# A decoder trunk with eight routed experts: four experts in 64 columns and two weight passes, heavy and light experts interleaved

## The chip, the cores and the metric

The kernel runs on one core of a Trainium2 chip. The metric is the device time of one execution in microseconds (us), as a median of several runs. The engines are named as the profile names them: PE is the tensor engine's matmul and PEld its weight load, DVE the vector engine, ACT the scalar engine, POOL the GpSimd engine, SP the engine whose queue issues nearly all transfers.

## The reference, cut to what matters

Two layers, each a mixer and then a feed-forward part, on 256 tokens of width 1024 in float32. The feed-forward part of layer 0 is dense, that of layer 1 is a mixture of eight experts of which each token takes two:

```
logits = t @ w_router                              # 256 x 8
top_v, top_i = top_k(logits, 2)
gates = sum(one_hot(top_i, 8) * softmax(top_v)[..., None], axis=1)
for e in range(8):
    out += gates[:, e:e+1] * ((silu(t @ w_g[e]) * (t @ w_u[e])) @ w_d[e])
```

Each expert has w_g and w_u of 1024 x 2816 and w_d of 2816 x 1024, 33 MiB in all. The 512 choices of the reference's own inputs fall on experts 0 to 7 as 60, 83, 83, 61, 59, 56, 66 and 44 tokens.

## The kernel before

The mixers and the dense part come first; the expert loop begins when the router has run, and takes most of the time.

**Precision.** A float32 product is made of three matmuls in the type fp32r. Every operand is split into a high part (a rounded copy, made by ACT) and a low part (what is left over, made by DVE); `mm3` (L158) then adds high x high, high x low and low x high into one PSUM bank.

**Blocks.** Weights come in blocks of 1 MiB (128 partitions x 2048 floats), 33 to an expert: 11 for gate, 11 for up, 11 for down. `weights` (L129) does everything for one block in the order of the program: a transfer on SP's queue into one of up to twelve buffers, ACT's copy `wr` (L117) and DVE's remainder `wl` (L119). Both `wr` and `wl` are in a pool `ring` of three buffers, so the split of a block can begin only when PE has finished the block three before it:

```
ring = ctx.enter_context(tc.tile_pool(name="ring", bufs=3))
```

One block feeds twelve matmuls of 512 columns (the last chunk's gate and up blocks feed 24 of 256).

**An expert.** `gather` (L714) picks the tokens of a pair of experts by matmuls with one-hot matrices, 128 columns to each expert, and splits the picked columns. `up` (L752) runs over six chunks c of the hidden width (five of 512, one of 256): tokens are the stationary operand (128 x 128), weights the moving one. ACT takes the SiLU of gate (`s`, L769), DVE multiplies it with up (`hh`, L771). One chunk later `turn` (L774) transposes `hh` on PE and splits it into `hr` and `hl`, and `down` (L785) multiplies with w_d into two banks that live for the whole expert. At the end `scale` (L799) applies the gate factor and `finish` (L809) scatters the rows back into `h` (`cb` L816 on PE, an addition L818 on DVE).

**Order.** The loop (L834) takes experts 0 to 7 and chunks 0 to 5 in order; between the gate half and the up half of a chunk it calls `turn` for the chunk before, after the up half `down`. Engines run their queues in order. A block that runs only if an expert has more than 128 tokens (`rest`, L852) is not entered with these inputs.

Of the kernel before, what the change touches and what calls it, by code (L numbers as in the profile page):

```python
# [16 lines left out]
P = 128  # L17
# [6 lines left out]
NE = 8  # L24
EPS = 1e-6
LEVELS = (64, 32, 16, 8, 4, 2, 1)
NL = len(LEVELS) + 1

# [6 lines left out]
K_ID, K_IOTA, K_LT, K_PAR = 0, 128, 384, 448  # L35
# [8 lines left out]
def small_arrays(i):  # L44
# [13 lines left out]
    c[:, K_LT:K_LT + NE * NE] = (e[None, :] < e[:, None]).reshape(1, -1)  # L58
    masks = np.zeros((P, NL, P), np.float32)
# [45 lines left out]
def trunk_kernel(ctx: ExitStack, tc: tile.TileContext, x, w_in, w_out, dense_w_gate, dense_w_up, dense_w_down,  # L105
# [62 lines left out]
    def tmp(shape, name, tag="tmp", bufs=5, dt=F32):  # L168
        pool = area["scratch"] if tag in ("tmp", "u", "cf_acc", "S", "r", "v", "gy", "qk", "sx") else sb
        return pool.tile(shape, dt, name=name, tag=tag, bufs=3 if tag == "tmp" and area["spare"] else bufs)  # L170
# [16 lines left out]
    iota, lt = kc[:, K_IOTA:K_IOTA + T], kc[:, K_LT:K_LT + NE * NE]  # L187
    wrt = kc[:, K_RT:K_M].rearrange("p (k e) -> p k e", e=NE)
# [431 lines left out]
    def moe(l, j, accs):  # L620
# [58 lines left out]
        gr = tmp([P, TT, NE, 2], "gr", tag="rt_g", bufs=1)  # L679
        nmax = tmp([P, 1], "nmax", tag="rt_n", bufs=1, dt=I32)  # L680

        def gates():
# [18 lines left out]
        X = {}  # L701

        def factors(p):
            oh = X[p][2]
            b = bank([P, 2, 2], "rgb")
            for i in range(2):
                for tt in range(TT):
                    nc.tensor.matmul(b[:, i], oh.bitcast(F32)[:, tt, i], gr[:, tt, 2 * p + i],
                                     start=(tt == 0), stop=(tt == TT - 1))
            rg = tmp([P, 2, 2], "rg", tag="rg", bufs=2)  # L710
            nc.vector.tensor_copy(rg, b)
            X[p].append(rg)

        def gather(p):  # L714
            oh = tmp([P, TT, 2, P], "oh", tag="oh", bufs=1, dt=F32R)
            for tt in range(TT):
                for i in range(2):
                    e = 2 * p + i
                    put = nc.vector.tensor_scalar(oh[:, tt, i], iota[:, 0:P], pos[:, tt, e:e + 1], None, op0=ALU.is_equal)
            xgr, xgl = pair("xg", "A" if p % 2 == 0 else "E")  # L720
            for k2 in range(KT // 2):
                b = bank([P, 2, 2 * P], "gb")
                for i in range(2):
                    kt = 2 * k2 + i
                    n = 0
                    for tt in range(TT):
                        for xs in (xr, xl):
                            nc.tensor.matmul(b[:, i], xs[:, tt, kt * P:(kt + 1) * P], oh[:, tt],  # L728
                                             start=(n == 0), stop=(n == 3))
                            n += 1  # L730
                for i in range(2):
                    kt = 2 * k2 + i
                    last = split(b[:, i], xgr[:, kt], xgl[:, kt], scale=col(R_FFN + KT * l + kt))
            X[p] = [xgr, xgl, oh]
            if p == 0:
                hold(2, (msk_set, last_x), (put,))
                with behind((put,)):
                    gates()
            else:
                factors(p)  # L740

        def back(p):
            oh = X[p][2]
            pt = tmp([P, 2, T], "pt", tag="pt", bufs=1, dt=F32R)
# [5 lines left out]
            X[p].append(pt)  # L750

        def up(e, c, mid):  # L752
            xgr, xgl = X[e // 2][0:2]
            ss = slice((e % 2) * P, (e % 2 + 1) * P)
            n = 512 if c < 5 else 256
            kn = 2048 // n
            bs = []
            for src in (gw, uw):
# [3 lines left out]
                for k0 in range(0, KT, kn):  # L762
                    wr, wl = weights(src[e, 2 * c + k0 // kn], kn, n)
# [3 lines left out]
            rg = X[e // 2][3][:, e % 2, 1:2]  # L767
# [220 lines left out]
```

## Time and profile before

| what | value |
|---|---|
| median of 3 runs | 1246.97 us (1246.82 to 1247.52) |
| the profiled execution | 1244.85 us, of which its span is 1242.7 us |
| mean granted PE clock | 0.994 of full speed |
| busy in the span: PE, DVE, ACT | 1212.8, 1009.7, 795.2 us |
| first and last matmul of gate or up in the expert loop | 444.2 and 1219.6 us |

The span is the time from the first to the last instruction that the profiler recorded. Busy times of different engines overlap. PE's busy time comes from matmuls whose ends are modelled: a matmul of 0.39 us overlaps the next one, which starts sooner than that.

### The profile page before, as it was taken

What the parts mean: (1) busy time and instruction counts of PE and PEld (TensorE: products, weight loads), DVE (VectorE), ACT (ScalarE), POOL (GpSimd) and SP (SyncE); (2) the same over time, 40 slices, a digit from 0 to 9 for tenths busy, and PEclk for the clock granted to TensorE, in tenths of its full rate; (3) what the DMA queues carried; (4) which work ended last, traced back from release to release, by engine and by line L of the source; (5) the groups of instructions that cost most, each with busy time, mean ns of one, the idle gap of its engine ahead of it and who ended that gap; (6) DMA issues with size and microseconds to landing.
All of it is one profiled execution on the core that took longest, in us unless ns stands there. A gap on an engine that the chain in (4) does not pass through costs nothing.

```text
span 1242.7 us, 17120 instructions
## 1 busy us (share of the span) xinstructions
PE 1212.8 (98%) x6897; PEld 1047.1 (84%) x6897; DVE 1009.7 (81%) x1032; ACT 795.2 (64%) x754; POOL 20.4 (2%) x31
## 2 busy tenths in 40 slices
PE   7999999999899999999999999999999999999996
PEld 6998999999899878888888888887787888888885
DVE  5987655555798778889889888888888898888986
ACT  6634543434554677777777777777777777677673
POOL 2000000000000000000000000000000000000000
PEclk9999999999999989999999999999999999999998
DMA  8434454545344769979799999899999899999971
GB/s 359 153 141 153 169 200 175 199 174 172 132 150 174 289 233 368 368 275 367 294 363 364 360 360 343 329 348 361 346 353 366 316 338 388 346 355 367 366 264 36
DMA packets 48788, 348.44 MB, mean 280 GB/s; under 512 B 5431, under 2 KB 5431, under 8 KB 6976
## 3 DMA queue, kind: packets, MB, share of 16 engines
q1 hardware_dynamic: 48384, 345.49, 74.2%
q0 software_dynamic: 320, 1.80, 0.4%
q8 instruction: 56, 0.92, 0.3%
q14 instruction: 28, 0.23, 0.0%
HBM read 346.23 MB, written 1.05 MB: 279 GB/s over the span
## 4 chain that ended last, share of the span: by engine, by line
PE 94%; DVE 4%; issue 1%; ACT 0%; DMA 0%; POOL 0%; POOLq 0%; SPq 0%; DVEq 0%
PE gu L160 16%; PE gu L161 16%; PE gu L159 16%; PE acc_y L160 9%; PE acc_y L159 9%; PE acc_y L161 9%; DVE wl L119 3%; PE gb L728 1%; PE tb L777 1%; PE sbk L417 1%; PE cb L816 1%; PE a_ps L166 1%; PE db L374 1%; PE vb L159 1%; PE vb L160 1%; PE vb L161 1%
## 5 line engine op out<-in xcount | busy, mean ns | idle before, releaser
L117 ACT ACTIVATE wr<-w 128x2048 fp32r<-128x2048 f32 (+2 forms) x273 | 403.9, 1496 | 224.5 <-issue 109.0
L119 DVE TENSOR_TENSOR wl<-w,wr 128x2048 fp32r<-128x2048 f32 (+2 forms) x273 | 475.8, 1765 | 77.4 <-ACT wr L117 77.2
L160 PE MATMUL gu<-wl,xg 128*128 128x512 f32 (+1 forms) x768 | 289.0, 376 | 2.5 <-DVE wl L119 2.4
L159 PE MATMUL gu<-wr,xg 128*128 128x512 f32 (+1 forms) x768 | 288.8, 376 | 0.0
L161 PE MATMUL gu<-wr,xg 128*128 128x512 f32 (+1 forms) x768 | 286.0, 372 | 0.0
L119 DVE TENSOR_TENSOR wl<-wx,wr 128x2048 fp32r<-128x2048 f32 x112 | 253.9, 2288 | 27.4 <-ACT wr L117 27.4
L117 ACT ACTIVATE wr<-wx 128x2048 fp32r<-128x2048 f32 x112 | 214.6, 1917 | 53.7 <-PE gu L161 26.4
L160 PE MATMUL acc_y<-wl,hr 128*128 128x512 f32 x440 | 174.8, 397 | 0.0
L161 PE MATMUL acc_y<-wr,hl 128*128 128x512 f32 x440 | 173.6, 394 | 0.0
L160 PEld LDWEIGHTS gu<-wl,xg 128*128 128x128 f32 x768 | 144.8, 188 | 29.2 <-DVE wl L119 5.7
L159 PE MATMUL acc_y<-wr,hr 128*128 128x512 f32 x440 | 166.1, 395 | 0.0
L159 PEld LDWEIGHTS gu<-wr,xg 128*128 128x128 f32 x768 | 144.7, 188 | 25.4
L161 PEld LDWEIGHTS gu<-wr,xg 128*128 128x128 f32 x768 | 144.7, 188 | 24.5
L160 PEld LDWEIGHTS acc_y<-wl,hr 128*128 128x128 f32 x440 | 82.8, 188 | 21.6 <-DVE wl L119 3.6
L161 PEld LDWEIGHTS acc_y<-wr,hl 128*128 128x128 f32 x440 | 82.9, 189 | 18.5
L159 PEld LDWEIGHTS acc_y<-wr,hr 128*128 128x128 f32 x440 | 82.6, 189 | 18.2
L159 PE MATMUL gu<-f,wr 128*128 128x256 f32 x336 | 95.1, 283 | 0.0
L160 PE MATMUL gu<-f,wr 128*128 128x256 f32 x336 | 95.0, 283 | 0.0
L161 PE MATMUL gu<-f,wl 128*128 128x256 f32 x336 | 95.0, 283 | 0.0
L160 PEld LDWEIGHTS gu<-f,wr 128*128 128x128 f32 x336 | 64.4, 192 | 0.4
L159 PEld LDWEIGHTS gu<-f,wr 128*128 128x128 f32 x336 | 64.4, 192 | 0.4
L161 PEld LDWEIGHTS gu<-f,wl 128*128 128x128 f32 x336 | 64.4, 192 | 0.0
(269 smaller groups left out, 1418.5 us busy)
## 6 DMA issues: line engine op xcount, KB each, us to landing
w<-in_moe_w_up_dram SPq DMA_DIRECT2D x52, 1024.0 KB, 7.2
w<-in_moe_w_down_dram SPq DMA_DIRECT2D x47, 1024.0 KB, 7.1
w<-in_moe_w_gate_dram SPq DMA_DIRECT2D x44, 1024.0 KB, 7.1
wx<-in_moe_w_gate_dram SPq DMA_DIRECT2D x39, 1024.0 KB, 7.2
wx<-in_moe_w_down_dram SPq DMA_DIRECT2D x39, 1024.0 KB, 7.3
wx<-in_moe_w_up_dram SPq DMA_DIRECT2D x34, 1024.0 KB, 7.1
w<-in_w_in_dram SPq DMA_DIRECT2D x20, 1024.0 KB, 4.9
w<-in_dense_w_gate_dram SPq DMA_DIRECT2D x11, 1024.0 KB, 4.9
```

The costliest lines, as they stand in the source:

```text
L117: i0 = nc.scalar.activation(r, src, AF.Copy, scale=scale)
L119: i1 = nc.vector.tensor_tensor(l, src, r.bitcast(F32), op=ALU.subtract)
L159: nc.tensor.matmul(o, sr, mr, start=start, stop=False)
L160: nc.tensor.matmul(o, sr, ml, start=False, stop=False)
L161: nc.tensor.matmul(o, sl, mr, start=False, stop=stop)
L166: nc.tensor.matmul(o, s[:, kt], m[:, kt], start=(n == 0 and kt == 0), stop=(n == 2 and kt == KT - 1))
L374: nc.tensor.matmul(db[:, o0:o1], la_t[n], mst[:, s0:s0 + o1 - o0], start=(n == 0), stop=(n == 1))
L417: nc.tensor.matmul(o, a0, a1, start=True, stop=True)
L728: nc.tensor.matmul(b[:, i], xs[:, tt, kt * P:(kt + 1) * P], oh[:, tt], start=(n == 0), stop=(n == 3))
L777: nc.tensor.transpose(b[:, i], hh[:, i * P:(i + 1) * P], ident)
L816: nc.tensor.matmul(cb, pt[:, e % 2, ts(tt)], ys[:, nh], start=(n == 0), stop=(n == 1))
```

## The change

On the chip, experts 1 to 7 are ranked by their token counts (`places`, 20 small DVE operations after two matmuls). The four with the fewest tokens become light; expert 0 and the other three are heavy. Places 0, 2, 4, 6 of the list hold heavy experts and 1, 3, 5, 7 light ones; place 0 is always expert 0. SP loads the expert number of each place from 1 to 7 into a register, and transfers take their address from it.

A light expert has 64 columns. Its stationary operand holds the high halves of 64 tokens beside the low halves, 128 columns in all. Two matmuls with `wr` and `wl` take the place of three, and the rows of the high and low halves come out apart. ACT copies gate and up from PSUM (`kept`); PE then multiplies each 128 columns of `kept` with `fold`, a 128 x 64 float32 matrix that adds the two halves, transposes them and applies the norm factor; SiLU, product and split follow on 64 columns.

Items are now pairs (place, chunk): three heavy ones first, then heavy and light ones in turn, three light ones last. The down product of a light item is put between the gate and the up half of the next light item. The temporary buffers `tmp` go from three to two. The fallback `rest` runs if a light expert has over 64 tokens or a heavy one over 128. The diff, cut:

```
+FEW = 64
+RANKS = (-1, 0, 4, 1, 5, 2, 6, 3)
+LAG = 3
...
-        return pool.tile(shape, dt, name=name, tag=tag, bufs=3 if tag == "tmp" and area["spare"] else bufs)
+        return pool.tile(shape, dt, name=name, tag=tag, bufs=2 if tag == "tmp" and area["spare"] else bufs)
...
+        def places():
             nb = bank([P, NE], "nb")
             for tt in range(TT):
                 nc.tensor.matmul(nb, oner, msk[:, tt], start=(tt == 0), stop=(tt == 1))
-            nc.vector.tensor_reduce(nmax, nb, axis=AX.X, op=ALU.max)
+            cnt = tmp([P, NE], "cnt", tag="rt_b", bufs=1)
+            nc.vector.tensor_copy(cnt, nb)
...
+            rank = tmp([P, NE], "rank", tag="rt_r", bufs=1)
+            nc.vector.tensor_reduce(rank, w0[:, :, 1:NE], axis=AX.X, op=ALU.add)
+            nc.vector.memset(rank[:, 0:1], -1.0)
...
+            for tt in range(TT):
+                for src, dst in ((pos[:, tt], placed[:, tt]), (gr[:, tt, :, 0], gp[:, tt, :, 0])):
+                    nc.vector.tensor_tensor(w0, to, src[:, None, :].broadcast_to([P, NE, NE]), op=ALU.mult)
+                    nc.vector.tensor_reduce(dst, w0, axis=AX.X, op=ALU.add)
...
+        def which(p):
+            expert[p] = nc.values_load(ids[0:1, p:p + 1], engines=(mybir.EngineType.SP,), min_val=0, max_val=NE - 1,
+                                       skip_runtime_bounds_check_because="a sum of one-hot rows times 0 to 7")
+
+        def block(src, p, n):
+            if p == 0:
+                return src[0, n]
+            return src[bass.ds(expert[p], 1), n].rearrange("e p n -> (e p) n")
...
+        def pick(p, c0, c1):
+            xg, oh = X[p][0:2]
             for k2 in range(KT // 2):
...
-                            nc.tensor.matmul(b[:, i], xs[:, tt, kt * P:(kt + 1) * P], oh[:, tt],
+                            nc.tensor.matmul(b[:, i, c0:c1], xs[:, tt, kt * P:(kt + 1) * P],
+                                             oh[:, tt].rearrange("p a b -> p (a b)")[:, c0:c1],
                                              start=(n == 0), stop=(n == 3))
...
+                    if c0 == 0:
+                        last = split(b[:, i, 0:P], xg[:, 0, kt], xg[:, 1, kt], scale=gain)
+                    if c1 > P:
+                        last = split(b[:, i, P:P + FEW], xg[:, 2, kt, 0:FEW], xg[:, 2, kt, FEW:P], scale=gain)
...
+                fold = tmp([P, FEW], "fold", tag="fold", bufs=2)
+                nc.vector.tensor_scalar(fold, folded, rg[:, 1:2], None, op0=ALU.mult)
...
         def up(e, c, mid):
...
-                        mm3(bs[-1], xgr[:, kt, ss], xgl[:, kt, ss], wr[:, i], wl[:, i], kt == 0, kt == KT - 1)
+                        if e % 2 == 0:
+                            mm3(bs[-1], xg[:, 0, kt], xg[:, 1, kt], wr[:, i], wl[:, i], kt == 0, kt == KT - 1)
+                        else:
+                            nc.tensor.matmul(bs[-1], xg[:, 2, kt], wr[:, i], start=(kt == 0), stop=False)
+                            nc.tensor.matmul(bs[-1], xg[:, 2, kt], wl[:, i], start=False, stop=(kt == KT - 1))
+                if e % 2 == 1:
+                    kept.append(tmp([P, n], "kept", tag="kept", bufs=2))
+                    nc.scalar.activation(kept[-1], bs[-1], AF.Copy)
...
+        def turn(e, c, hh, n):
...
+            b = bank([P, 2, nk, FEW], "fb")
+            for n in range(2):
+                for i in range(nk):
+                    nc.tensor.matmul(b[:, n, i], hh[n][:, i * P:(i + 1) * P], fold, start=True, stop=True)
+            s = tmp([P, nk, FEW], "s")
+            nc.scalar.activation(s, b[:, 0], AF.Silu)
+            nc.vector.tensor_tensor(s, b[:, 1], s, op=ALU.mult)
+            hb = tmp([P, nk, 2, FEW], "hb", tag="hr", bufs=2, dt=F32R)
+            area["turn"] = split(s, hb[:, :, 0], hb[:, :, 1])
...
+                    else:
+                        hb = hr[:, 2 * k2 + i].rearrange("p a b -> p (a b)")
+                        nc.tensor.matmul(Y[e][nh], hb, wr[:, i, cs], start=first, stop=False)
+                        nc.tensor.matmul(Y[e][nh], hb, wl[:, i, cs], start=False, stop=fin)
...
+        many = [(e, c) for e in range(0, NE, 2) for c in range(6)]
+        little = [(e, c) for e in range(1, NE, 2) for c in range(6)]
+        items = many[:LAG]
+        for a, b in zip(many[LAG:], little):
+            items += [a, b]
+        items += little[len(little) - LAG:]
...
+        def between(k, e, c):
             if (e, c) == (0, 0):
-                factors(0)
+                factors(0, 0)
+            if (e, c) == (0, 1):
+                limits(*places())
+                marks(0, 1)
+                pick(0, P, P + FEW)
+                factors(0, 1)
+                back(0)
+            if k:
+                pe, pc, ph, pn = done[-1]
+                held_back.append((pe, pc, turn(pe, pc, ph, pn)))
                 hold(2, area["turn"])
...
+        def lower(k, e, c, turned):
+            down(e, c, *turned)
+            if c == 5 and e < NE - 1:
+                todo.setdefault(("scale", k + 1), []).append(e)
+                todo.setdefault(("finish", k + 2), []).append((e, 0))
+                todo.setdefault(("finish", k + 3), []).append((e, 1))
...
+        for k, (e, c) in enumerate(items):
+            if c == 0 and e > 0:
+                which(e)
+
+            def mid(k=k, e=e, c=c):
+                ready = list(held_back)
+                held_back.clear()
+                between(k, e, c)
+                for pe, pc, turned in ready:
+                    lower(k, pe, pc, turned)
+
+            hh, n = up(e, c, mid)
+            done.append((e, c, hh, n))
+            for pe, pc, turned in [x for x in held_back if x[0] % 2 == 0]:
+                lower(k, pe, pc, turned)
+            held_back[:] = [x for x in held_back if x[0] % 2 == 1]
+            for pe, tt in todo.pop(("finish", k), ()):
+                finish(pe, (tt,))
+            if c == 5 and e % 2 == 0 and e < NE - 2:
+                p = e // 2 + 1
+                space(p)
+                marks(p, 0)
+                marks(p, 1)
+                pick(p, 0, P + FEW)
+                for i in range(2):
+                    factors(p, i)
+                back(p)
...
-    with tc.If(fullest > P):
+    with tc.If(fullest > 0):
```

## Rows read from the trace of the kernel before

**Rows 1.** The page's head, busy time of PE, and the chain that ended last, by engine.

```profile
span 1242.7 us, 17120 instructions
...
PE 1212.8 (98%) x6897; PEld 1047.1 (84%) x6897; DVE 1009.7 (81%) x1032; ACT 795.2 (64%) x754; POOL 20.4 (2%) x31
...
PE 94%; DVE 4%; issue 1%; ACT 0%; DMA 0%; POOL 0%; POOLq 0%; SPq 0%; DVEq 0%
```

**Rows 2.** Busy time of each engine in the expert loop, as one stretch.

```profile
core 0: us, PE busy (x) PEld busy (x) DVE busy (x) ACT busy (x) POOL busy (x), PEclk, DMA share, GB/s
444.00:1220.00 776.00, 773.46 (x3703) 641.04 (x3703) 679.88 (x447) 569.49 (x405) 0.59 (x1) 1.00 0.90 339
```

**Rows 3.** Timeline of PE, the first and last of 23 consecutive matmuls: start, length.

```profile
642.26 0.40 PE L160 MATMUL gu<-wl,xg 128*128 128x512 f32 x1
...
647.29 0.40 PE L161 MATMUL gu<-wr,xg 128*128 128x512 f32 x1
```

**Rows 4.** Groups by line and form: count, busy us, mean ns, idle before.

```profile
L119 DVE TENSOR_TENSOR wl<-w,wr 128x2048 fp32r<-128x2048 f32 x138 | 312.4, 2287 | 28.4 <-ACT wr L117 28.4
L117 ACT ACTIVATE wr<-w 128x2048 fp32r<-128x2048 f32 x139 | 266.2, 1917 | 63.7 <-PE gu L161 38.1 <-PE acc_y L161 20.5 <-DVE wl L119 1.7
...
L771 DVE SCALAR_TENSOR_TENSOR hh<-gu,rg,s 128x512 f32<-128x512 f32 x40 | 30.0, 749 | 15.6 <-PE gu L161 15.4
...
L119 DVE TENSOR_TENSOR hl<-tb,hr 128x512 fp32r<-128x512 f32 x40 | 27.4, 684 | 1.4 <-ACT hr L117 1.4
...
L117 ACT ACTIVATE hr<-tb 128x512 fp32r<-128x512 f32 x40 | 23.9, 597 | 38.3 <-PE tb L777 38.3
```

**Rows 5.** Timeline of DVE: two remainders back to back, two additions back to back.

```profile
659.01 4.50 DVE L119 TENSOR_TENSOR wl<-w,wr 128x2048 fp32r<-128x2048 f32 x2 [0.52 <-ACT wr L117]
...
668.85 1.28 DVE L818 TENSOR_TENSOR h<-h,cb 128x512 f32<-128x512 f32 x2
```

**Rows 6.** Timeline of ACT through one chunk, with what ended each wait.

```profile
655.99 0.69 ACT L769 ACTIVATE s<-gu,rg 128x512 f32<-128x512 f32 x1 [0.80 <-PE gu L161]
...
657.06 1.92 ACT L117 ACTIVATE wr<-w 128x2048 fp32r<-128x2048 f32 x1
659.18 1.92 ACT L117 ACTIVATE wr<-w 128x2048 fp32r<-128x2048 f32 x1 [0.20 <-PE gu L161]
661.90 1.92 ACT L117 ACTIVATE wr<-w 128x2048 fp32r<-128x2048 f32 x1 [0.81 <-PE gu L161]
664.69 1.92 ACT L117 ACTIVATE wr<-wx 128x2048 fp32r<-128x2048 f32 x1 [0.87 <-PE acc_y L161]
```

**Rows 7.** Chain in order of time: a pair's gather, a chunk's four transposes.

```profile
585.35 3.64 PE gb L728 x32
...
655.96 0.44 PE tb L777 x4
```

**Rows 8.** Timeline of PE, float32 matmuls outside the expert loop.

```profile
373.64 1.11 PE L417 MATMUL sbk<-E 64*128 64x64 f32 x16
...
431.20 3.64 PE L642 MATMUL lb<-wrg,ft 128*128 128x8 f32 x32
```

**Rows 9.** Timeline of DVE, small operations of the router.

```profile
436.06 0.29 DVE L667 TENSOR_REDUCE rk<-cmp 128x16 f32<-128x128 f32 x1
...
438.45 0.17 DVE L684 TENSOR_REDUCE mx<-L 128x2 f32<-128x16 f32 x1
```

**Rows 10.** SP's queue: what its transfers wait for, and one register load.

```profile
SPq L140 <- DVE wl L119: 1012.3, 307, 17.8
...
L954 SPq TENSOR_LOAD <-nmax x1: 482/482/482, 1199.0 to 1199.0; - x1
```

**Rows 11.** Three stretches of the expert loop, columns as in rows 2.

```profile
454.00:1204.00 750.00, 747.46 (x3559) 618.46 (x3559) 661.07 (x426) 548.80 (x387) 0.59 (x1) 1.00 0.93 350
...
1032.00:1040.00 8.00, 8.00 (x38) 6.63 (x36) 6.31 (x4) 6.58 (x5) 0.00 (x0) 1.00 1.01 418
1026.00:1123.00 97.00, 96.50 (x455) 79.11 (x455) 84.98 (x51) 70.81 (x48) 0.59 (x1) 1.00 0.95 364
```

More of the change, by code (lines that the diff above doesn't have):

```diff
@@ L714, in gather @@
-        def gather(p):
-            oh = tmp([P, TT, 2, P], "oh", tag="oh", bufs=1, dt=F32R)
-            for tt in range(TT):
[L717 to L720, printed above, removed]
+            cnt = tmp([P, NE], "cnt", tag="rt_b", bufs=1)
+            nc.vector.tensor_copy(cnt, nb)
+            w0 = cmp[:, 0, 0:NE]
@@ new lines, in moe @@
+        gw, uw, dw = moe_w_gate[j], moe_w_up[j], moe_w_down[j]
+        X, expert = {}, {0: 0}
+        def which(p):
[5 more added lines that the diff above has]
+            return src[bass.ds(expert[p], 1), n].rearrange("e p n -> (e p) n")
@@ L732, in gather, with space, factors @@
                     kt = 2 * k2 + i
[L733 to L740, printed above, removed]
+                    gain = col(R_FFN + KT * l + kt)
+                    if c0 == 0:
+                        last = split(b[:, i, 0:P], xg[:, 0, kt], xg[:, 1, kt], scale=gain)
+                    if c1 > P:
+                        last = split(b[:, i, P:P + FEW], xg[:, 2, kt, 0:FEW], xg[:, 2, kt, FEW:P], scale=gain)
+            return last
+        def space(p):
+            t = tmp([P, 4, KT, P], "xg", tag="A" if p % 2 == 0 else "E", bufs=1, dt=F32R)
+            X[p] = [t, t[:, 3, 0:4].rearrange("p (a b) n -> p a b n", a=TT), {}, t[:, 3, 4:8].rearrange("p (a b) n -> p a (b n)", a=2), {}]
+        def factors(p, i):
+            oh = X[p][1]
+            g = gr if p == 0 and i == 0 else gp
+            b = bank([P, 2], "rgb")
+            for tt in range(TT):
+                nc.tensor.matmul(b, oh.bitcast(F32)[:, tt, i], g[:, tt, 2 * p + i], start=(tt == 0), stop=(tt == TT - 1))
+            rg = tmp([P, 2], "rg", tag="rg", bufs=4)
+            nc.vector.tensor_copy(rg, b)
+            X[p][2][i] = rg
+            if i == 1:
+                fold = tmp([P, FEW], "fold", tag="fold", bufs=2)
+                nc.vector.tensor_scalar(fold, folded, rg[:, 1:2], None, op0=ALU.mult)
+                X[p][4][0] = fold
         def back(p):
-            oh = X[p][2]
-            pt = tmp([P, 2, T], "pt", tag="pt", bufs=1, dt=F32R)
+            oh = X[p][1]
+            pt = X[p][3]
             b = bank([P, 2, T], "ptb")
@@ L772, in up @@
-            return hh, n
-        def turn(hh, n):
-            b = bank([P, n // P, P], "tb")
-            for i in range(n // P):
-                nc.tensor.transpose(b[:, i], hh[:, i * P:(i + 1) * P], ident)
-            hr = tmp([P, n // P, P], "hr", tag="hr", bufs=2, dt=F32R)
-            hl = tmp([P, n // P, P], "hl", tag="hl", bufs=2, dt=F32R)
-            area["turn"] = split(b, hr, hl)
-            return hr, hl, n // P
+            nc.vector.scalar_tensor_tensor(s, bs[1], rg, s, op0=ALU.mult, op1=ALU.mult)
@@ L845, in moe @@
-        down(last[0], last[1], *turn(*last[2:]))
+        space(0)
+        put = marks(0, 0)
+        pick(0, 0, P)
+        hold(2, (msk_set, last_x), (put,))
+        with behind((put,)):
+            gates()
+        many = [(e, c) for e in range(0, NE, 2) for c in range(6)]
[4 more added lines that the diff above has]
+        items += little[len(little) - LAG:]
+        held_back, todo = [], {}
@@ L846, in moe @@
+        ready = list(held_back)
+        k = len(items)
+        pe, pc, ph, pn = done[-1]
+        ready.append((pe, pc, turn(pe, pc, ph, pn)))
+        for pe, pc, turned in ready:
+            lower(k, pe, pc, turned)
+        for key in sorted((q for q in todo), key=lambda q: (q[1], q[0] != "scale")):
+            for v in todo[key]:
+                if key[0] == "scale":
+                    scale(v)
+                else:
+                    finish(v[0], (v[1],))
         low = scale(NE - 1)
```

131 lines of the change are left out of this document (80 added, 51 removed).

## The prediction

> **What bounds the kernel now.** I read the page first. PE is busy for 98% of the span and holds 94% of the chain that ended last [rows 1]. The share is an average over stages, so I took the expert loop alone: in its 776 us PE is busy for 773.5, DVE for 679.9, ACT for 569.5, and the transfers run at 339 GB/s with a share of 0.90; the granted clock is 1.00 of full speed, the 2.4 GHz level [rows 2]. Since matmul ends are modelled, a busy PE need not be a full one, so I checked the pace: 23 matmuls start within 5.03 us, 0.229 us apart without a hole [rows 3]. A heavy block (12 matmuls) thus takes 2.74 us. A chunk of 512 has six blocks and four transposes. PE sets the pace now.
>
> The next question is what PE will wait for when it gets faster. A block costs ACT 1.92 and DVE 2.29 us [rows 4]; back to back two remainders take 4.50, so DVE's pace is 2.21 [rows 5]. The reader should see in ACT's timeline why these engines idle: nearly every `wr` waits 0.2 to 0.9 us for a matmul of PE [rows 6]. That is the ring of three: a slot comes free when PE is done with a block, and then 0.2 (the wait's release) + 1.92 + 2.29 + some 0.1 = 4.5 us pass until PE can use the new block in it, while PE works on the two blocks between. Two heavy blocks last 5.48, so 1.0 us is to spare, and PE does not stall. Two light blocks (8 matmuls, 1.83 us each) last 3.66: the ring is then late. DVE's 2.21 is above 1.83 as well. This is the heart of the forecast.
>
> **The change part by part.** *PE's work.* Four light experts of 33 blocks drop 4 of 12 matmuls: 4 x 33 x 4 x 0.229 = 121 us less. (The 256-column blocks drop 8 of 24 at about half the time each; I count them alike.)
>
> The turn of a light chunk gets dearer. Four transposes take 0.44 us [rows 7]. Now 8 float32 products take their place, with a 128-row, 128-column stationary and 64 moving columns. The trace has none of that form. Float32 products show up as two PE instructions each: the router's 16 products are 32 rows in 3.64 us, 0.11 each with 8 columns; the mixer's 64-column products on half the rows are 16 in 1.11, at most 0.07 apart [rows 8]. I take 0.11, since those use the full 128 rows as `fold` does: 16 x 0.11 = 1.76 per chunk, and per expert 88 x 0.11 - 22 x 0.11 = 7.3, in four experts 29 us. The low end, 0.07, would cost 15 in all, so 14 us less; the high end is PE's pace for 512 columns, 0.229, 42 us more.
>
> The first pair's tokens are now picked in two goes. The gather of a pair is 32 matmuls in 3.64 us [rows 7], and 0.11 is also what the 8-column ones cost, so the second go costs about 3.6. PE's work falls by 121 - 29 - 4 = 88 us.
>
> *The ring.* PE's order follows from the text. Around one heavy item H and one light item L it is: gate HH, fold, up HH, then gate LL, transposes, down LL, up LL, then down HH. So six heavy blocks alternate with six light ones, too long a run for a ring of three to even out. Let t = 0 be the first light matmul; durations are those of [rows 4 to 6]. L1 and L2 are ready (L2 at 1.7). `hh` of the heavy chunk follows on DVE (0.75, to 2.35). L3: its slot is free at 0.2, ACT to 2.1, DVE 2.3 to 4.57; PE is past L2 and the transposes at 4.1 and starts at 4.6. L4: DVE to 6.8, starts then. `hl` of the heavy chunk on DVE to 7.4. L5: DVE to 9.6; L6: to 11.8; the next heavy block: to 14.0. Without waiting PE would be there at 6 x 1.83 + 0.44 = 11.4. So a light run loses 2.6 us, a wait of PE for `wl`. In the heavy run DVE needs 6 x 2.21 + about 0.8 (product and split of 64 columns, half the size of `hh` and `hl`) = 14.1 of 18.2 us and catches up, but cannot lay in more than two blocks. Per chunk pair: 33.8 us before, 29.6 by PE's work, 32.2 with the loss.
>
> 21 light items are interleaved, three of them short (chunk 5). 18 full runs cost 18 x 2.6 = 47. The three short ones (three blocks): L3 is ready at 4.6, `hh` and `hl` add 0.5 and 0.4, the next block is ready at about 7.3 against 5.9, so 1.4 each, 4 in all. The last three items are light alone: a chunk costs DVE 6 x 2.21 + 0.8 = 14.1 against PE's 11.0 + 1.76 = 12.7, together 3. Bounds for a full run: with `hh` and `hl` both outside the chain it loses 2.6 - 1.3 = 1.3. With ACT's extra copies in it (`kept` twice and `hr`, 0.6 to 0.7 each by the SiLU of the same size [rows 6] and `hr` [rows 4]) it loses 2.6 + 2.0 = 4.6.
>
> *The ranking.* `places` is emitted in the middle of item 1, and PE's next work, the pick of the light tokens, needs it. 20 DVE operations on 64 elements lie between 0.17 (16 elements) and 0.29 (128) [rows 9]; at 0.23 and 0.03 between two, 5.2, and with `nb` and the one-hot marks about 6 us of PE standing still. It is 0 if these run earlier, in DVE's idle time; 10 if each waits for the one before it a tenth longer and the pick's splits are waited for too. I take 6. What is queued behind on DVE are the next `wl`; two blocks lie ready, so nothing else is late.
>
> *Additions and scatter.* `yg` falls into heavy runs, where DVE has room. Of each of seven experts one half of `finish` falls at the head of a light run: two additions, 1.28 [rows 5], against PE's four scatter matmuls at 0.23: 0.4 each, 3 in all. The splits of three gathers now stand directly before a light run; against a gather's 3.64 on PE [rows 7] eight of some 0.5 on DVE and the marks are about 1 us more each. I take 6 together; 0 to 12.
>
> *At nothing.* Register loads on SP: seven at 0.48 us; SP spends 1012 us waiting for `wl`, so they hide there [rows 10]; without that cover 3.4 us. ACT gains some 25 us of copies over 569 of 776; what hides them is its wait for PE; what they cost without that is the slower rival below. PSUM: the accumulators of two experts hold four of eight banks all the time, and gate, up and the turn of two items share four; each is held 4 to 9 us of 32. `tmp` with two buffers holds one tile of each kind of item. The fallback: the ranked counts are 44, 56, 59, 61, all within 64.
>
> **Sum.** 88 - 47 - 4 - 3 - 6 - 6 = 22 us off the profiled execution, 1244.85 to about 1223. The median of the runs is 2.1 above that execution, so 1247 - 22 = 1225.
>
> **The rivals.**
>
> *PE's work decides.* If the ring's loss vanishes (blocks of both kinds mixed more finely on PE than I read it), 88 - 12 = 76 goes: 1171; 1160 to 1204 with the bounds. For it: DVE's and ACT's sums still fit. Against it: ACT's wait for a slot in nearly every block [rows 6] and a ring that is not changed.
>
> *Slower: the light run costs more than the third pass gives.* The place is the light run, the mechanism ACT in order: `kept` of gate, `hr` and `kept` of up stand between the `wr` of L4 and of the next heavy block. If each delays DVE fully, the loss is 4.6 a run: 18 x 2.0 = 36 more, 1261. It decides from 2.6 + 22/18 = 3.8 us a run on. For it: a wait of ACT on PE stands before `s` and `hr` already (38.3 us over 40 `hr` [rows 4]). Against it: ACT's block is 0.37 shorter than DVE's, so part of it hides.
>
> *The transfers become the bound.* The part of the loop with steady transfers moves 750 us x 350 GB/s = 262.5 MB; the best stretch of one expert ran at 364 GB/s [rows 11]. If that is all they can do, 721 us remain of 750: 29 less, 1218. Against it: 418 GB/s over 8 us in the same loop with all engines busy [rows 11]; at 376 (350 over the share of 0.93) 698 remain, and they don't bind before 52 us are won. The Trainium skill (HBM Reference, Specifications (TRN2)) gives a core some 358 GB/s when its pair streams too, and more to one alone; by 358 as a cap, 733 us would remain and the time would be 1230. The trace's 418 shows that this cap does not hold here.
>
> *It does not do what it says.* Should a light expert have over 64 tokens, the fallback streams all weights again, over 700 us more (264 blocks of 1.05 MB at 376 GB/s). The counts speak against it.
>
> **How the numbers follow.** The ring-limited gain 50% (1205 to 1240), PE's work 20%, transfers 8%, no change 6%, slower by ACT 14%, fallback 2%. I predict 1225. The range leaves out the lower half of the PE case, half of the slower case and the fallback: 1172 to 1254. About 0.2% (2.5 us) is what a measurement of this kernel can tell from no change. Faster 0.50 + 0.20 + 0.08 = 0.78, same 0.06, slower 0.16.
>
> **What would show it.** In the profile after: L runs of PE with waits for DVE `wl` in every light chunk, some 2.6 us; DVE without idle there, but waiting for ACT, and ACT for PE, in heavy runs; `fb` 16 instructions, 0.11 apart; one stop of PE of about 6 us near 460 before `gb`; transfers at 360 to 370 GB/s. I am wrong if light runs flow without waits (then 1171), if `fb` is much dearer or cheaper, or if PE stops at new places, such as bank waits at gate.

## The result, and the profile after

The changed kernel takes 1296.4 us (four runs, 1296.3 to 1296.5) against 1246.9 us: a ratio of 1.040, 95% interval 1.038 to 1.041. It is slower by 49.5 us, where 22 us faster was forecast; 1225 missed by 71 us, and the range's upper end, 1254, by 42.

The page after, its head, busy time of PE, DVE and ACT, and the chain that ended last:

```profile
span 1294.7 us, 17231 instructions
...
PE 1180.2 (91%) x6633; PEld 996.7 (77%) x6633; DVE 1004.9 (78%) x1098; ACT 806.3 (62%) x834; POOL 20.3 (2%) x31
...
PE 70%; DVE 18%; ACT 5%; issue 5%; DMA 1%; POOL 0%; SPq 0%; ACTq 0%; DVEq 0%; POOLq 0%
```

PE lost its hold on the chain: 70% in place of 94% [rows 1], and DVE's share went from 4% to 18%. The work did fall (6633 matmul rows for 6897). Next the expert loop after, by windows: the whole, an undisturbed stretch, the first gather, the ranking (columns as in [rows 2]).

```profile
444.00:1280.00 836.00, 748.61 (x3480) 597.29 (x3480) 680.75 (x515) 582.20 (x486) 0.59 (x1) 0.96 0.82 314
620.00:720.00 100.00, 94.98 (x444) 75.54 (x443) 89.27 (x54) 75.88 (x56) 0.00 (x0) 1.00 0.96 375
580.00:590.00 10.00, 5.68 (x37) 4.98 (x36) 7.75 (x15) 5.20 (x14) 0.00 (x0) 0.79 0.73 301
590.00:600.00 10.00, 9.59 (x34) 7.82 (x35) 4.27 (x10) 6.16 (x10) 0.00 (x0) 0.70 0.05 8
460.00:465.00 5.00, 4.76 (x22) 3.53 (x20) 5.00 (x4) 2.97 (x3) 0.00 (x0) 1.00 0.60 231
465.00:470.00 5.00, 0.59 (x4) 0.59 (x4) 4.73 (x24) 0.53 (x1) 0.00 (x0) 0.97 0.99 385
470.00:480.00 10.00, 10.00 (x46) 9.71 (x46) 3.45 (x14) 4.10 (x11) 0.00 (x0) 0.51 0.15 63
```

Three things are to be seen. The span is 52 us longer with the same DVE time in the loop (680.8 for 679.9; this window is 60 us longer than that of before, since it takes in more of the end). PE stands for 87 us of it, where it stood for 2.5. And the granted clock, 1.00 throughout the loop before [rows 2], has a mean of 0.96: over 836 us that is some 33 us' worth of PE at full clock, an upper bound of its cost, since part of it falls where PE stands. Behind a stop PE runs on at the lower level, 1.2 GHz: after the one at 465 to 470 the clock is 0.51 for ten us in which PE counts as fully busy. That busy time is slow, not full. The Trainium skill (TensorE: Matmul & The Clock Gate, Part 1) puts it as "the default state is throttled, and activity releases the throttle"; the rows agree, with 0.51 behind the stop and 1.00 again in the stretch from 620 us.

ACT's timeline through the light run that ends near 769 us, after:

```profile
754.55 0.60 ACT L842 ACTIVATE kept<-gu 128x512 f32<-128x512 f32 x1 [1.85 <-PE gu L839]
755.04 5.50 ACT L121 ACTIVATE wr<-w 128x2048 fp32r<-128x2048 f32 x3
761.50 1.91 ACT L121 ACTIVATE wr<-wx 128x2048 fp32r<-128x2048 f32 x1 [0.95 <-PE acc_y L889]
768.67 0.60 ACT L842 ACTIVATE kept<-gu 128x512 f32<-128x512 f32 x1 [5.26 <-PE gu L839]
769.17 5.51 ACT L121 ACTIVATE wr<-wx 128x2048 fp32r<-128x2048 f32 x3
```

ACT stands 5.26 us before `kept`, waiting for PE's end of the up half, and then makes three `wr` in a row: at least one of their slots had been free while it stood, as the tied run below shows. DVE then waited 2.21 us for the first of them:

```profile
766.61 2.28 DVE L123 TENSOR_TENSOR wl<-wx,wr 128x2048 fp32r<-128x2048 f32 x1
771.10 2.29 DVE L123 TENSOR_TENSOR wl<-wx,wr 128x2048 fp32r<-128x2048 f32 x1 [2.21 <-ACT wr L121]
```

The waits of ACT and PE in the whole loop say the same (us in total, times, longest):

```profile
ACT kept L842 <- PE gu L839: 73.6, 28, 5.5
ACT s L867 <- PE fb L865: 49.6, 20, 2.8
...
PE gu L839 <- DVE wl L123: 27.3, 30, 1.8
PE acc_y L890 <- DVE wl L123: 20.0, 26, 1.6
PE acc_y L164 <- DVE wl L123: 15.4, 13, 1.6
```

### The profile page after: what moved, and what is told of

It is laid out like the page before. It is cut to its first block, busy times and chain, and to the rows that moved or that the text cites. A ratio compares the mean times of both kernels' runs of the same rounds, so it can differ in the third digit from the quotient of the medians.

```text
span 1294.7 us, 17231 instructions
## 1 busy us (share of the span) xinstructions
PE 1180.2 (91%) x6633; PEld 996.7 (77%) x6633; DVE 1004.9 (78%) x1098; ACT 806.3 (62%) x834; POOL 20.3 (2%) x31
## 3 DMA queue, kind: packets, MB, share of 16 engines
HBM read 346.23 MB, written 1.05 MB: 268 GB/s over the span
## 4 chain that ended last, share of the span: by engine, by line
PE 70%; DVE 18%; ACT 5%; issue 5%; DMA 1%; POOL 0%; SPq 0%; ACTq 0%; DVEq 0%; POOLq 0%
DVE wl L123 15%; PE gu L164 9%; PE gu L163 9%; PE gu L165 9%; PE acc_y L164 5%; PE acc_y L165 5%; PE acc_y L163 5%; ACT wr L121 4%; PE gu L839 4%; PE gu L838 3%; PE fb L865 3%; PE sbk L422 1%; PE a_ps L170 1%; PE gb L782 1%; PE cb L911 1%
## 5 line engine op out<-in xcount | busy, mean ns | idle before, releaser
L839 PE MATMUL gu<-wl,xg 128*128 128x512 f32 (+1 forms) x384 | 151.1, 400 | 27.9 <-DVE wl L123 27.3
L838 PE MATMUL gu<-wr,xg 128*128 128x512 f32 (+1 forms) x384 | 148.1, 391 | 1.0 <-ACT wr L121 1.0
L164 PE MATMUL gu<-wl,xg 128*128 128x512 f32 (+1 forms) x384 | 145.6, 379 | 1.0 <-DVE wl L123 1.0
L163 PE MATMUL gu<-wr,xg 128*128 128x512 f32 (+1 forms) x384 | 145.7, 379 | 0.0
L165 PE MATMUL gu<-wr,xg 128*128 128x512 f32 (+1 forms) x384 | 143.7, 374 | 0.0
L164 PE MATMUL acc_y<-wl,hr 128*128 128x512 f32 x264 | 106.6, 404 | 15.5 <-DVE wl L123 15.4
L839 PEld LDWEIGHTS gu<-wl,xg 128*128 128x128 f32 x384 | 75.5, 197 | 58.1 <-DVE wl L123 45.1
L165 PE MATMUL acc_y<-wr,hl 128*128 128x512 f32 x264 | 104.2, 395 | 0.0
L163 PE MATMUL acc_y<-wr,hr 128*128 128x512 f32 x264 | 99.3, 395 | 1.3 <-ACT wr L121 1.3
L165 PE MATMUL gu<-f,wl 128*128 128x256 f32 x336 | 95.0, 283 | 0.0
L838 PEld LDWEIGHTS gu<-wr,xg 128*128 128x128 f32 x384 | 76.2, 198 | 15.4 <-ACT wr L121 2.2
L890 PE MATMUL acc_y<-wl,hb 128*128 128x512 f32 x176 | 69.0, 430 | 20.1 <-DVE wl L123 20.0
L164 PEld LDWEIGHTS gu<-wl,xg 128*128 128x128 f32 x384 | 73.0, 190 | 14.4 <-DVE wl L123 2.2
L163 PEld LDWEIGHTS gu<-wr,xg 128*128 128x128 f32 x384 | 73.1, 190 | 12.9
L165 PEld LDWEIGHTS gu<-wr,xg 128*128 128x128 f32 x384 | 72.9, 190 | 12.6
L164 PEld LDWEIGHTS acc_y<-wl,hr 128*128 128x128 f32 x264 | 49.7, 188 | 33.6 <-DVE wl L123 23.3
```

The source lines that it names most:

```text
L163: nc.tensor.matmul(o, sr, mr, start=start, stop=False)
L164: nc.tensor.matmul(o, sr, ml, start=False, stop=False)
L165: nc.tensor.matmul(o, sl, mr, start=False, stop=stop)
L838: nc.tensor.matmul(bs[-1], xg[:, 2, kt], wr[:, i], start=(kt == 0), stop=False)
L839: nc.tensor.matmul(bs[-1], xg[:, 2, kt], wl[:, i], start=False, stop=(kt == KT - 1))
L890: nc.tensor.matmul(Y[e][nh], hb, wl[:, i, cs], start=False, stop=fin)
```

## The experiments

Five theories stand against each other. *Order*: in ACT's queue `kept` (and `s` of the fold) waits for PE in front of `wr` whose slots are free. *Ring*: runs of six light blocks lose what a ring of three must lose. *DVE*: its own work is the pace. *Start, banks*: the ranking and the gathers stop PE. *Clock*: each stop costs more than its length.

Where only one time stands, it is one run beside a run of the kernel before on the same chip (1245.5 to 1247.6 us). The 1296.4 us of the changed kernel was measured apart from the variants, so a difference of 2 or 3 us between single runs says nothing. Line numbers of a variant differ by a few from those of the changed kernel.

**The third pass put back in light experts.**

```
-        nc.tensor.matmul(bs[-1], xg[:, 2, kt], wl[:, i], start=False, stop=(kt == KT - 1))
+        nc.tensor.matmul(bs[-1], xg[:, 2, kt], wl[:, i], start=False, stop=False)
+        nc.tensor.matmul(bs[-1], xg[:, 2, kt], wr[:, i], start=False, stop=(kt == KT - 1))
...
```

> The light experts get a third matmul again for each block (the pass with `wr` is done twice, so that the result is another); ranking, 64 columns, fold and order stay. PE's work grows by 4 x 33 x 4 x 0.229 = 121 us. If PE's work sets the light runs: 1296 + 121 = 1417 us. Ring theory: a light block lasts 2.74 us again, two of them 5.48 against the 4.5 us of a refill, so PE waits no more and the third pass fills what was waiting: 1300 to 1340 us. Then the rest over the kernel before (1247) is what fold (29), start (16), gathers and light tail add.

1316.2 us: 121 us of matmuls cost 20 us. Of what the two-pass product saves on PE, 101 us were waiting in disguise; PE's waits for `wl` at `gu` in the light runs are gone (0.7 us in total, where they were 27.3). So PE's work no longer set the pace.

**Two passes alone, in the kernel before.** `mm3` of odd experts becomes two matmuls, in `up` and `down`.

> The kernel before, with its order, its 128 columns and without ranking and fold; only the third pass (low x high) of the odd experts is left out, so the result is another. PE's work falls by 121 us. PE theory: 1246 - 121 = 1125 us. Ring and DVE theory: a light chunk cannot be faster than DVE's 6 x 2.21 + 0.75 + 0.68 = 14.7 us against 16.9 before, 2.2 us x 22 chunks = 48 us less: 1195 to 1205 us.

1230.6 us, 17.1 us less than the run of before beside it, for 121 us of work: even without ranking, fold and exchange a seventh of it arrives, and less than DVE's pace allows. A miss for both theories. Here too ACT waits in front of a copy out of PSUM, `hr`, and PE for `wl`:

```profile
ACT hr L117 <- PE tb L781: 65.1, 34, 3.8
PE gu L770 <- DVE wl L119: 45.4, 38, 2.3
```

DVE is busy for 85 to 93 of each 100 us there, from 500 us on.

**Copies `kept` moved.** First the up's copy on DVE, then both copies later in the text, then tied behind a `wr`:

```
-                    nc.scalar.activation(kept[-1], bs[-1], AF.Copy)
+                    nc.vector.tensor_copy(kept[-1], bs[-1])      # up half only
```

> The copy of the light item's up half (`kept`) moves from ACT to DVE; all else as in the changed kernel (1296.4 us). Order theory: in ACT's queue this copy waits for the last light matmul and holds back the `wr` of slots that are already free; with it gone from ACT, `wr` runs ahead of that wait, but DVE then waits at the same place in its own order, so only part of the loss comes back: 1265 to 1285 us. Ring theory: the light runs lose what a ring of three must lose, whatever stands in ACT's queue: 1293 to 1300 us. DVE theory: DVE's pace sets the light runs, and 18 copies of some 0.7 us more make it slower: 1305 to 1310 us.

1282.1 us, in the order theory's range.

> Both copies `kept` of a light item stay on ACT but are put behind the blocks of the next heavy down product in its order, so ACT never stands before a `wr` to wait for the end of a light half. Order theory: the waits of ACT for `gu` (28 waits, 73.6 us in the changed kernel) no longer delay a block; a cycle of a heavy and a light chunk goes from some 35.1 to 33 us, 18 x 2 = 36 us and the clock that the stops cost on top: 1245 to 1262 us. Ring theory: 1293 to 1300 us, as the slots come free no sooner. If gate and up banks held longer make PE wait for a bank: slower, above 1300 us.

1295.7 us: no answer. ACT's waits for `gu` are as they were (71.3 us, 28 times); the sequence of its queue had not changed, but for two `hr`, since a planner and not the text orders it.

```
+            if e % 2 == 1:
+                t = tmp([P, n], "kept", tag="kept", bufs=2)
+                with behind(area["last"][:1]):
+                    nc.scalar.activation(t, hh[1], AF.Copy)
...
```

> The order of ACT's queue is set by a planner, not by the text: moving `kept` in the text alone changed nothing (1295.7 us). Here the two copies `kept` of each light item are tied behind a `wr`: the gate's copy behind the last `wr` of the down product that follows it, the up's behind the last `wr` of the next heavy down product. In the changed kernel's queue the up's copy stands before the second of these two in some ten of the chunk pairs, and after it in the others. Order theory: the pairs whose cycle takes 34.7 to 39.3 us fall towards the 32.4 us of the others; of some 31 us above 32.4 in them, gathers and scatters keep a third: 1270 to 1282 us. Ring theory: 1293 to 1300 us.

1269.8 us, 26.6 us off, as the order theory had it. The same place in ACT's timeline, with the copies tied:

```profile
759.43 1.92 ACT L121 ACTIVATE wr<-wx 128x2048 fp32r<-128x2048 f32 x1 [0.31 <-PE acc_y L890]
762.21 1.91 ACT L121 ACTIVATE wr<-wx 128x2048 fp32r<-128x2048 f32 x1 [0.86 <-PE gu L842]
765.83 0.60 ACT L975 ACTIVATE kept<-gu 128x512 f32<-128x512 f32 x1 [1.71 <-PE gu L843]
766.33 1.91 ACT L121 ACTIVATE wr<-wx 128x2048 fp32r<-128x2048 f32 x1
```

One `wr` has passed in front of the copy, and the wait of 5.26 us has become 1.71. In the whole loop ACT's waits for `gu` before `kept` fall from 73.6 to 33.0 us, and PE's waits for `wl` in the heavy down products from 15.4 to 0.8. From one heavy gate to the next, this pair takes 39.81 us in the changed kernel and 34.98 in the tied one:

```profile
736.07 0.39 PE L163 MATMUL gu<-wr,xg 128*128 128x512 f32 x1
775.88 0.28 PE L163 MATMUL gu<-wr,xg 128*128 128x256 f32 x1
```

```profile
736.35 0.39 PE L163 MATMUL gu<-wr,xg 128*128 128x512 f32 x1
771.33 0.28 PE L163 MATMUL gu<-wr,xg 128*128 128x256 f32 x1
```

**The ranking.**

```
-            return src[bass.ds(expert[p], 1), n].rearrange("e p n -> (e p) n")
+            return src[SEAT[p], n]          # SEAT = (0, 7, 6, 5, 1, 4, 2, 3)
...
-                limits(*places())
```

> The ranking, the reordering of positions and factors and the register loads are left out: the list of places is written into the kernel for these inputs (0, 7, 6, 5, 1, 4, 2, 3), addresses are constants, the fallback's limit is a zero. The second pick stays where it is. Start theory: the ranking's chain on DVE and its stop of PE cost the 16 us by which the changed kernel is behind at 478 us, less some 5 for the pick itself, and the registers nothing: 1283 to 1288 us. Register theory: addresses from registers delay transfers all along: 1270 us or less. Rival: the second pick with its splits makes the stop, and the ranking hides in it: 1292 to 1297 us.

1286.2 us. Then the same ranking one item earlier:

> The ranking (`places` and `limits`) is emitted one item earlier, in the middle of item 0; the pick of the light tokens stays in item 1. Start theory: the 20 small operations on DVE then run where PE has work before it, and the stop of PE near 465 us shrinks as with the fixed list (1286.2 us): 1284 to 1290 us. Rival: the planner puts them at the same place again or in front of the first `wl`, so the stop only moves: 1293 to 1300 us.

1291.4 us, just outside the first range: half of what the fixed list gives comes back. The fixed list also drops the register addresses and the reordering; what the other half is was not separated.

**The gathers.** Two halves, and the filling of PE's stop:

```
-                pick(p, 0, P + FEW)
+                pick(p, 0, P + FEW, (0, 1))
...
+            if c == 2 and e % 2 == 1 and e < NE - 1:
+                pick(e // 2 + 1, 0, P + FEW, (2, 3))
...
```

> On top of the tied copies (1269.8 us): each pair's gather is done in two goes, the first half of the width after the last heavy chunk as now, the second half after the light chunk that follows; factors and transposes of the marks come after the second. Bank theory: the gather fills four banks at once while the other four hold accumulators, so PE's next product stands still until the splits have emptied one (5.2 us at 586 in the tied kernel, then a stretch at half clock); with two banks a go PE finds a free bank: 5 to 8 us for each of three gathers, 1246 to 1256 us. Rival: the 16 splits cost DVE and ACT their time wherever they stand and PE waits for blocks in its place: 1264 to 1272 us.

1255.3 us: 14.5 us off, 4.8 for each gather. PE's waits of `rgb` for a split, 9.4 us in the tied kernel, are gone; the factors come later here too, behind the second half.

> On top of the tied copies (1269.8 us): in the three gathers PE computes the third bank four times and the fourth three times (40 more matmuls, some 4.6 us each gather), so that it stands still for less; nothing else. Clock theory: the granted clock, 0.5 for some 10 us after each gather, stays at 1.00 and gives back 4 to 5 us each, less under 1 us by the later last bank: 1256 to 1262 us. Rival: PE is not what limits there (next to no transfers run in these 10 us, the blocks are late anyway): 1267 to 1274 us, with the clock at 1.00.

1260.3 us, with 120 matmuls more. The first gather, in the tied kernel and then filled:

```profile
580.00:590.00 10.00, 6.10 (x54) 5.96 (x53) 7.67 (x12) 6.31 (x11) 0.00 (x0) 1.00 0.85 335
590.00:594.00 4.00, 2.85 (x13) 2.32 (x13) 2.09 (x10) 1.82 (x6) 0.00 (x0) 0.52 0.46 188
594.00:600.00 6.00, 6.00 (x23) 4.87 (x22) 1.34 (x3) 3.83 (x7) 0.00 (x0) 0.75 0.01 3
```

```profile
580.00:590.00 10.00, 10.00 (x91) 10.00 (x89) 7.59 (x12) 6.36 (x12) 0.00 (x0) 1.00 0.85 342
590.00:600.00 10.00, 8.07 (x35) 6.59 (x35) 4.01 (x12) 5.92 (x12) 0.00 (x0) 0.83 0.12 47
```

In the tied kernel PE is busy for 6.10 of the first ten us, and the clock is 0.52 from 590 to 594 and 0.75 from 594 to 600. Filled, PE's stop before 590 is gone, and the ten us after it have 0.83. With useless work added, the kernel is 9.5 us faster (one run each), so the lower clock is a cost of its own, some 3 us a gather; it did not stay at 1.00, as its expectation had it.

**The three together; the plain order.**

> The tied copies, the early ranking and the gather in halves together. If the three losses are separate, it comes to the sum: 1296.4 - 26.6 - 5 - (15 to 24) = 1241 to 1250 us. If the stops share a limit (DVE's own work), less: 1255 to 1262 us.

1249.8 us: the three losses add up (26.6 + 14.5 + 5.0 = 46.1, measured 46.6), and what they leave is no faster than before.

> The tied copies, and the items in plain order (all six chunks of an expert before the next), in place of heavy and light in turn. DVE theory: light chunks then run at DVE's 14.1 to 14.7 us against 16.9 of a heavy one, as in the kernel with two passes only (1230.6 us), plus ranking and picks (10 to 17), fold hidden under DVE: 1240 to 1256 us. Theory that only the exchange lets DVE catch up in heavy chunks: PE idles in light experts and loses clock: 1275 to 1300 us.

1264.0 us, between the two: 5.8 us off the exchange with the same tie, so the exchange of heavy and light items itself earned nothing with the gathers as they were. The plain order with the gathers in halves (1255.3 us with the exchange) was not run.

**Ring of four, and its control.**

```
+        if area["spare"] is not None and area["count"] % 4 == 0:
+            r = area["spare"].tile([P, a, b], F32R, name="wr", tag="wr4", bufs=1)
...
-            w = area["spare"].tile([P, a, b], F32, name="wx", tag="wx", bufs=4)
+            w = area["spare"].tile([P, a, b], F32, name="wx", tag="wx", bufs=2)
```

> Every fourth block's `wr` and `wl` go to a fourth pair of buffers, so that a slot is used again after four blocks, not three; its room is taken from the transfers' buffers, of which there are seven, not nine, in the steady part. Ring theory: three light blocks last 5.5 us against a refill of 4.5, so the light runs lose only what DVE's pace costs, under 1 us each in place of 2.6: 18 x 2 = 36 us less, 1255 to 1265 us. Order theory: a fourth slot gives ACT one more block of lead but `kept` still stands in front: 1270 to 1285 us. If the transfers need the nine buffers: 1300 us or more.

> The changed kernel with seven buffers for transfers, not nine, in the steady part, and the ring of three: the control for the ring of four, which took the room of the two (1301.6 us). If the transfers need the nine: 1315 to 1330 us, and the ring of four gained the rest. If nine are more than are needed: 1294 to 1299 us, and the ring of four lost 5 us by itself, its slots freed no sooner because ACT's order holds them.

1301.6 and 1299.7 us. The two buffers less cost some 3 us, which is near what single runs can tell, and the fourth slot gave nothing. ACT still waited before `kept`, 91.7 us in 36 waits with the ring of four, so a freer slot was of no use to it; that this is the whole reason is argued. A ring of four with the copies tied was not tried.

**The fold's tail late, and POOL.**

> On top of the three repairs (tied copies, early ranking, gather in halves: 1249.8 us): SiLU, product and split of the folded light chunk (`s`, `hb`) are tied behind the last `wr` of the heavy item's up half. There ACT waited 47.7 us in 20 waits for `fb` with free slots behind it, and DVE was 1.4 us idle for ACT just before the light run. Order theory: the light run then begins with one more block laid in, up to 2 us for each of some 18 runs: 1215 to 1235 us. DVE theory: in the light run DVE is busy without a hole (844.8 to 863.4 us), and what it gains before the run is only its 1.4 us of idle time there: 1232 to 1246 us. Rival: the later `hb` delays the light down product or holds banks: 1250 us or more.

1255.1 us (ratio to before 1.007, 1.005 to 1.009), 5 us worse than without (1249.8, one run). ACT's 47.7 us of waiting for `fb` are gone, but its waits before `wr` (`gu`, L165) rose from 21.8 to 42.0 us and those before the heavy `s` to 28.1: the wait moved, and nothing was won.

> As the run before it, and every eighth block's remainder `wl` is computed by POOL, which stands idle, in place of DVE: 33 x 2.21 = 73 us less of DVE's work in the loop. DVE theory: the light runs are DVE's, 0.75 of a block less in each run of six, and more lead before it: 15 to 30 us less than the run before. Rival: POOL's remainder takes over 6 us (no row shows one) or slows DVE beside it: the block is late and the gain is none or negative.

> The kernel before with every eighth remainder on POOL and nothing else. PE theory: PE sets the pace there, DVE has room; no change, 1244 to 1248 us. If POOL's remainder takes longer than the 1.0 us that the ring has to spare, each of 33 blocks stops PE for the rest: 1260 us or more, and the row of POOL gives its length.

1302.4 us (1.046, 1.044 to 1.047), 47 us more than the kernel with the late fold under it, and 1290.4 us, 44 more than the kernel before. POOL's and DVE's timelines in the kernel before with POOL helping:

```profile
622.03 4.64 POOL L119 TENSOR_TENSOR wl<-wx,wr 128x2048 fp32r<-128x2048 f32 x1 [24.32 <-ACT wr L117]
```

```profile
618.15 2.29 DVE L121 TENSOR_TENSOR wl<-w,wr 128x2048 fp32r<-128x2048 f32 x1 [0.80 <-ACT wr L117]
...
624.05 4.77 DVE L121 TENSOR_TENSOR wl<-wx,wr 128x2048 fp32r<-128x2048 f32 x1 [3.01 <-ACT wr L117]
```

POOL takes twice as long as DVE's 2.29 us, and the remainder that DVE begins beside it ends only 2.15 us after POOL's, as if it had waited for POOL's end (626.67).

**Two by two.** A pair of items on PE as gate H, gate L, up H, down L, down H, up L, two blocks each; in the second version also the factors ahead of the gather and `LAG = 2`.

```
+            if hv:
+                bgh = half_of(gw, *hv)
...
+            if li:
+                bgl = half_of(gw, *li)
...
+            if hv:
+                buh = half_of(uw, *hv)
...
+            if tl:
+                lower(le, lc, tl)
...
+            if oldh:
+                lower(oldh[0], oldh[1], th)
...
+            if li:
+                bul = half_of(uw, *li)
```

> The changed kernel with another order on PE: of a heavy and a light item the two gate blocks of the heavy one, two of the light one, two up blocks heavy, two down blocks light, two down blocks heavy, two up blocks light, so that never more than two light blocks follow each other; with it the early ranking, the gather in halves, the copies and the fold's tail tied behind the `wr` before which ACT would wait. Work and operations are those of the changed kernel. Ring theory (the loss comes from runs of six light blocks, which a ring of three cannot even out): a slot is free for two or more other blocks, one of them heavy, 4.57 us against 4.5; a cycle falls from some 34 us (1249.8 us as a whole with the repairs) to 30 to 31.5, 21 x 3 = 63 us: 1180 to 1205 us. DVE theory (its 12 x 2.21 + 2.3 = 28.8 us a cycle and its waits set the pace anyway): 32 to 33 us a cycle, 1220 to 1240 us. Rival (banks: gate, up, fold and transposes of two items at once in four banks stop PE): 1245 us or more.

> As the two-by-two order (1241.1 us), with two more edits. The factors and the transposes of the marks come before a pair's gather, not after it: there PE waited up to 3.4 us for `rg` on DVE, behind the splits, in each of three gathers, with the clock falling after it; 3 to 6 us each. And two heavy chunks, not three, go ahead, so that two light chunks, not three, stand alone at the end: one heavy chunk of 16.9 and one light one of some 16 alone become a pair of 31, 2 us. Together 1221 to 1231 us. If the transfers (367 to 374 GB/s in the steady part) or DVE take the gain back: 1236 to 1243 us.

1241.1 us (0.996, 0.995 to 0.998) and 1235.3 us (0.992, 0.990 to 0.993): the last is faster than both kernels, by 0.8% than the one before. Both contain the repairs above, and the fold's tail tied late. The first lies a little above the DVE theory's range, the second between its two. Windows of the second: the loop, a part with little else than cycles, one with a gather.

```profile
444.00:1220.00 776.00, 722.57 (x3486) 584.85 (x3485) 677.80 (x518) 580.01 (x489) 0.59 (x1) 0.99 0.89 342
600.00:700.00 100.00, 94.64 (x456) 76.12 (x455) 89.98 (x64) 77.78 (x66) 0.00 (x0) 1.00 0.96 366
700.00:800.00 100.00, 92.45 (x452) 75.07 (x451) 87.17 (x66) 72.93 (x63) 0.00 (x0) 0.98 0.94 356
```

In the steady part PE is busy for 95%, DVE for 90%, and the transfers for 96% at 366 GB/s: three limits within a few per cent. The changed kernel's undisturbed stretch, 620 to 720 us, was there already (95%, 89%, 96% at 375 GB/s).

## Why the prediction was wrong

**The fold's term was right, and the place of the ranking's stop.** `fb` is 16 instructions 0.11 us apart, and there is one stop of PE before the second pick, near 465, as forecast. One chunk's `fb` after, count and first and last start:

```profile
L865 PE MATMUL fb<-fold,kept x16: 217/275/275, 647.4 to 649.0; 128*128 128x64 f32 x16
```

**The light run was mis-sized: ACT's order was left out of its chain.** From one heavy gate to the next (the first after a down product), a pair of full chunks takes 32.3 to 33.8 us where the up's `kept` stands behind both `wr` of the next heavy down product; 32.2 was worked out, so the ring's own term came out near. Where `kept` stands before the second `wr`, which is so in ten pairs of the later loop, the five full ones among them take 35.5 to 39.8 us; with the copies tied the same five take 33.8 to 35.0. PE's waits for `wl` in light items are 39.9 us in the tied kernel (26.7 at `gu`, 13.2 at `acc_y`), near the 47 of the sum. This is the step that failed most: the light run was costed with ACT's copies outside the chain. The slower rival named the mechanism (ACT in order, `kept` before `wr`) and was given 14% and 36 us; the tied copies measured 26.6. "Part of it hides" was wrong there, because ACT does not only spend 0.6 us on the copy, it waits up to 5.5 us for it.

**The gathers were mis-sized.** "About 1 us more each" was 4.8 each that the halves gave back. The reason was costed at nothing: four banks for gate, up and turn. A gather fills all four, and PE stands until a split has emptied one. In the kernel before, the accumulators of one expert take two banks, not four, and PE stands for 2.5 us in the whole loop [rows 2], its gathers included. PE's timeline after, at the second pick (for the next paragraph) and at the first gather:

```profile
469.41 1.72 PE L782 MATMUL gb<-xg,xt 128*128 128x64 f32 x8 [4.61 <-DVE xg L768]
...
579.79 3.29 PE L782 MATMUL gb<-xg,xt 128*128 128x192 f32 x28
586.98 1.98 PE L804 MATMUL rgb<-gp,xg 128*128 128x2 f32 x8 [3.90 <-DVE xg L125]
```

**The ranking was mis-sized, less so.** 6 us of stop was 4.6 by its row; the whole start cost more, since PE then ran at half clock. From 444 us to the end of the pick the kernel fell 16.3 us behind against some 10 (6 for the ranking, 3.6 for the pick). (The up half of the second chunk starts at 478.41 us, before at 462.07.) But 2.7 of the 16.3 were lost ahead of the ranking's stop, in the first three halves, where PE's clock was lower in the changed kernel. The same window before, then after:

```profile
445.00:450.00 5.00, 5.00 (x26) 4.17 (x24) 2.32 (x10) 4.03 (x5) 0.00 (x0) 1.00 0.03 13
```

```profile
445.00:450.00 5.00, 5.00 (x16) 4.10 (x16) 1.27 (x4) 1.10 (x3) 0.00 (x0) 0.58 0.11 44
```

No run separates why. The ranking's chain itself was as worked out, 0.26 us a step and 4.3 us in all, the first two and the last of it on DVE:

```profile
466.33 0.21 DVE L716 TENSOR_TENSOR cmp<-cnt 128x64 f32<-128x64 f32 x1
466.58 0.23 DVE L717 SCALAR_TENSOR_TENSOR cmp<-cmp,kc 128x64 f32<-128x64 f32 x1
...
470.37 0.21 DVE L732 TENSOR_REDUCE gp<-cmp 128x8 f32<-128x64 f32 x1
```

**The clock was left out.** Every stop was costed at its own length, on a trace in which the loop runs at 1.00 [rows 2]. The repairs' gains contain it; only the filled gather shows it by itself.

**What stays open.** Of 71 us the three repairs return 46.6. Mixing two by two and mending it return 14.5 more. That gain has in it whatever the long light runs lost, the 47 us of the sum too, so it does not tell how much of the miss was theirs. The last 10 us, from 1235 to 1225, were not separated. That transfers, DVE or ACT's waits keep them is argued from the windows above, not shown.

The rival of the transfers is open. The changed kernel moves 314 GB/s as a mean of the loop, but 375 from 620 to 720 us, with a DMA share of 0.96, so the 364 of [rows 11] is no cap. Yet the forecast's own pair of 32.2 us, 12 blocks of 1.05 MB, needs 391 GB/s (an estimate from these numbers), which the prediction did not set beside the transfers' pace; the mended kernel holds 366 from 600 to 700 us. "PE's work decides" fell: the finer mix that was its condition was built, and it gave 1241, not 1171.

## What to carry to other kernels

When the engine that sets the pace gets faster, cost the in-order queues that feed it from their own timeline: a 0.6 us copy that waits for the end of a stage costs what it holds back, and its place in the queue must be read in the trace, since the text need not set it. Before taking work from an engine at 98%, look at the second one: with DVE at 88% and transfers at 0.93 of their time, some 7 to 12% was all there was to win (an estimate that leaves their work as it is), however much PE work goes. Where PE used to run without a hole, add to each new stop the stretch at the lower clock behind it, and count the PSUM banks at every burst.

## What the runs showed of the hardware that was not expected

A remainder on POOL takes 4.64 us in the row above, and DVE's remainder beside it 4.77 in place of 2.29; in the kernel before with POOL helping, DVE's mean rose to 2.51 us. The Trainium skill (SBUF — State Buffer, SBUF: two separate sides) calls the port pair of the two an exclusive lock, with the other one blocked for the whole instruction; the rows agree. Forty more matmuls in each of three gathers made a kernel 9.5 us faster, because PE's clock fell less.
